# Attention's last product in plain fp32, with its transposed weights copied once

## The chip, the cores and the metric

The kernel runs on one core of a Trainium2 chip. A core has a matrix engine (TensorE, PE in the profile, its weight loads PEld), a vector engine (VectorE, DVE), an activation engine (ScalarE, ACT), a general engine (GpSimd, POOL) and an engine that issues most transfers (SyncE, SP). Each takes its instructions in the order in which the program wrote them, and waits on semaphores for the others. Matmul results land in PSUM, which VectorE and ScalarE read; the rest of the on-chip data is in SBUF. The metric is the time of one execution on the device, in microseconds (us), as the median of several runs.

## What is computed

A network of two layers on 1040 tokens (16 learned ones ahead of 1024 of the input) with 1024 features, all in fp32. Layer 0 mixes tokens by two parallel parts, a stick-breaking attention of 8 heads of 64 features and a state-space model (S5) with a gated unit behind it; layer 1 mixes by a gated delta rule; each layer ends in a wide MLP with squared ReLU. The change touches the attention alone:

```python
def block(args):
    qb, bi = args
    q_pos = bi * SB_BLOCK + jnp.arange(SB_BLOCK)
    valid = (key_pos[None, :] < q_pos[:, None]) & (key_pos[None, :] >= pad)
    z = jnp.einsum('bhqd,bhkd->bhqk', qb, kh) * scale
    log_keep = jnp.where(valid, jax.nn.log_sigmoid(-z), 0.0)
    log_surv = lax.cumsum(log_keep, axis=3, reverse=True) - log_keep
    w = jnp.exp(jnp.where(valid, jax.nn.log_sigmoid(z) + log_surv, -jnp.inf))
    return jnp.einsum('bhqk,bhkd->bhqd', w, vh)
```

The last line, weights times values, is what the change does in another way.

## The kernel before

**Number format.** Large products run in fp32r, a form of fp32 that TensorE multiplies at reduced precision. To keep fp32 accuracy each operand is split exactly into a part `hi`, rounded to fp32r, and a remainder `lo`, and three products hi x hi, hi x lo and lo x hi are summed in PSUM (`unit`, lines 174 to 176; the split itself is `split`, lines 222 to 230, a cast on ScalarE and a subtraction on VectorE or GpSimd). A few small products, those of S5 among them (lines 674, 715, 717), run in plain fp32 without a split.

**Order of the work.** `mixer0` (line 955) writes the program of layer 0. A main strand makes the S5 inputs, the values, the queries and keys, then calls `attention`, then the output product. Side strands (the four quarters of S5, `s5_quarter`, and the gated unit `glu` with the first half of the output product) are generators; `tick` writes a piece of them after each unit of the main strand, and some of them pause until a rough count of TensorE's time, `self.clock`, has gone on by so much. So each engine's order is fixed when the program is built, and S5 and the gated unit are interleaved with the attention.

**Attention.** Heads are taken in four pairs p (128 features, one tile), queries in four pairs pr of tiles of 128 (the 16 extra tokens go with the first pair). That makes 4 x 4 x 2 = 32 units (p, pr, head). For each unit `weights` (line 828) makes the scores with three products (lines 845 to 847) and a mask (849), takes two sigmoids of them on ScalarE (851, 852), runs a reversed running product along the keys on VectorE (853), and multiplies the two on VectorE or GpSimd (854). The weights are then [queries, keys]. Four units later (`AHEAD` = 4) `outputs` (line 866) takes them up:

- The keys go by blocks (the 16 extra tokens, then 128 each): 2 pr + 3 blocks for a unit, in groups of one and then two, pr + 2 groups, so 8 x (2 + 3 + 4 + 5) = 112 groups in all.
- `group` transposes the weights of its blocks on TensorE into a PSUM tile `tr` (line 881; there are three such tiles).
- ScalarE rounds the transposed weights to `th` (line 890), VectorE makes the remainder `tl` (line 891). Both are scratch tiles from a ring of ten.
- `products` multiplies them by the values. The values of a block lie as 64 columns of hi beside 64 of lo, so one product of the 128 columns with `th` gives hi x hi in 64 partitions and lo x hi in the other 64 (line 899), and a second one, of the 64 hi columns with `tl`, adds to the former (line 900). `later` holds a group's products back behind the transposes of the next three groups (`DEP` = 3).
- `store` copies one half of the result on ScalarE (line 913) and adds the other on VectorE (line 914).

`load_v` (line 811) fetches the values of a pair of heads into a raw buffer (`wraw`, two of them, which all weight loads share) and splits them, hi on ScalarE, lo on GpSimd. For the next pair it is called ahead of the last unit of the present one.

Of the kernel before, what the change touches and what calls it, by code (L numbers as in the profile page):

```python
# [44 lines left out]
def f(ap):  # L45
    return ap.bitcast(F32)


class Net:
# [6 lines left out]
    def step(self, strand):  # L56
        """emit the next piece of a strand; whether there was one that need not wait"""
        self.busy, was = True, self.busy
        going = False
        while strand:  # L60
            try:
                going = next(strand[0]) is not WAIT
                break
            except StopIteration:
                strand.pop(0)
        self.busy = was
        return going

    def tick(self, n=1):
        """emit n more pieces of the work that runs beside the present one, of its strands in turn"""  # L70
# [24 lines left out]
    def until(self, name, strand=None):  # L95
        """emit of a strand, or of all, up to what is named"""
        while name not in self.done:
            if strand is None or not self.step(strand):
                self.clock += 0.5
                self.tick()  # L100
# [12 lines left out]
    def pause(self, us):  # L113
        """wait while the tensor engine is given work for some time"""
# [35 lines left out]
    def weight(self, src, n=1024, spare=False, fast=False):  # L150
        """a weight tile as hi + lo; spare: in slots, beside the weights in use"""
# [15 lines left out]
    def unit(self, pt, kts, wap, rhs, o, n):  # L167
        """One output tile [128, n]: three passes of split products over kts."""
# [25 lines left out]
    def rowscale(self, cols, n, nsub, invd):  # L194
        """cols(j): [128, sub] summands whose sum over partitions is wanted per token; returns
        1/sqrt(sum * invd + eps) in a PSUM tile [128, nsub * sub], the same in every partition."""
# [10 lines left out]
    def spread(self, r, sub, nsub):  # L207
        """[sub, nsub] per-token values to rows that every partition holds."""
# [13 lines left out]
    def split(self, hi, lo, src, gain=None, lo_eng=None):  # L222
        """hi + lo = src (* gain per partition) exactly."""
# [8 lines left out]
    def norm_in(self, st, m, c, chunks, hsn, gcol):  # L232
        """Account one piece of the residual stream for the next product: its square sum, and the
        piece times the norm's gain as hi + lo."""
# [21 lines left out]
    def pieces(self, src, c, chunks, eng, mid=None):  # L256
        """a chunk of a [128, 8, tokens] stream, some feature tiles to a slot"""
# [11 lines left out]
    def first_norm(self):  # L269
        """the first norm, of all but the first chunk in pieces beside the first product"""  # L270
# [29 lines left out]
    def residual(self, acc, ssq, reuse, gpost, hs_old, gpre, chunks):  # L300
        """hs + rms(acc) * gain, and what the next norm or the output takes of it. Returns a hook for
        the last product before it, which goes by chunks of tokens: a chunk is taken up while the next
        one is made. reuse gives its place to the next state."""
# [65 lines left out]
    def mlp(self, layer, st, hs_d, chunks, gpre, ahead=None):  # L369
        """gpre: the next norm's gain column, or None at the end."""  # L370
# [79 lines left out]
    def s5_params(self):  # L450
# [24 lines left out]
        # powers 0..8 of exp(lambda dt), [128, 9, 16]  # L475
# [17 lines left out]
        # decay of a chunk and its rotation, as unit vectors 1, 2, 4 .. 128 chunks on  # L493
# [14 lines left out]
        # coef = (abar - 1) / lambda  # L508
# [15 lines left out]
        # bbar over b, -c_re and -c_im beside c  # L524
# [17 lines left out]
        # rotation tables over chunks, pairs 0..7 and 8..15  # L542
# [30 lines left out]
    def s5_mats(self, q):  # L573
        """Matrices of the groups 8 q .. 8 q + 7 for chunks of 8 tokens: inputs to state, inputs to
        outputs, and the state before the chunk to outputs."""
# [34 lines left out]
        # impulse response, then the Toeplitz matrices by reading it at shifted places  # L610
# [22 lines left out]
    def s5_ready(self, ud):  # L633
        """what the quarters need, back on chip, a quarter ahead"""
# [30 lines left out]
    def s5_quarter(self, q, ud):  # L665
# [21 lines left out]
        def rotate(dst, src, sign):  # L687
            """dst = src * exp(sign i phi)"""
# [59 lines left out]
    def glu(self):  # L748
        """gelu(y) * sigmoid(gelu(y) w + b), in place, with its square sum"""
# [34 lines left out]
    def normed(self, tiles, ssq, gcol, reuse=None):  # L784
        """rms norm over the features of 4 tiles, as hi + lo"""
# [11 lines left out]
    def attention(self, qd, kd, vd, vd0):  # L797
        """stick-breaking attention, by pairs of heads (a tile of features) and pairs of query tiles"""
# [12 lines left out]
        def load_v(p):  # L811
            cols = slice(128 * p, 128 * p + 128)
            raw = self.raw()
            nc.sync.dma_start(raw[:, :1024].rearrange("p (k d) -> p k d", k=8), vd[:, :, cols].rearrange("k p d -> p k d"))
            r0 = self.small([16, 128], "v0r", bufs=1)
            nc.sync.dma_start(r0, vd0[:, cols])
            # for a head and a block of keys, hi beside lo
            v0 = self.small([16, 2, 2, 64], "v0", F32R)
            self.split(v0[:, :, 0], v0[:, :, 1], r0.rearrange("p (h d) -> p h d", h=2), lo_eng=nc.gpsimd)
            V = []  # L820
            for h in range(2):
                t = self.slot("vv", F32R)
                t4 = t[:, :1024].rearrange("p (k s d) -> p k s d", k=8, s=2)
                self.split(t4[:, :, 0], t4[:, :, 1], raw[:, :1024].rearrange("p (k h d) -> p k h d", k=8, h=2)[:, :, h], lo_eng=nc.gpsimd)
                V.append([v0[:, h].rearrange("p s d -> p (s d)")] + [t[:, 128 * i:128 * i + 128] for i in range(8)])
            return V

        def weights(qk, h, i, kp=None, sg=None):
            """[q, keys] weights of q tile i"""
# [27 lines left out]
        pend = []  # L857
        self.ssq_sb = self.slot("ssqsb")

        def later(item, depth=DEP):  # L860
            """products wait for their operands behind the transposes of the next groups"""
# [4 lines left out]
        def outputs(p, pr, h, w, V, osb):  # L866
            # blocks of keys: (index, first q column, q columns)
# [4 lines left out]
            def group(gr):  # L872
# [16 lines left out]
                th, tl = self.tmp("wth", F32R), self.tmp("wtl", F32R)  # L889
                nc.scalar.copy(th[:kn, :off], pt[:kn, :off])  # L890
                v.tensor_sub(tl[:kn, :off], pt[:kn, :off], f(th[:kn, :off]))

                def products():
# [3 lines left out]
                    for kb, c0, cn, at in place:  # L897
                        a, o = V[h][kb], av[0][:, c0:c0 + cn]
                        nc.tensor.matmul(o, a, th[:kn, at:at + cn], start=first, stop=False, skip_group_check=True)
                        nc.tensor.matmul(o[:64], a[:, :64], tl[:kn, at:at + cn], start=False, stop=kb == 2 * pr + 2 or c0 == 256, skip_group_check=True)  # L900
# [8 lines left out]
            def store():  # L909
                t0 = TT[2 * pr + 1][0]  # L910
                hp = slice(64 * h, 64 * h + 64)
                for t, c0, cn in ((t0, 0, 256), (0, 256, 16))[:2 if pr == 0 else 1]:
                    nc.scalar.copy(osb[hp, t:t + cn], av[0][0:64, c0:c0 + cn])
                    v.tensor_add(osb[hp, t:t + cn], av[0][64:128, c0:c0 + cn], osb[hp, t:t + cn])
# [40 lines left out]
    def mixer0(self, st, rows):  # L955
# [3 lines left out]
        # s5 inputs  # L959
# [22 lines left out]
        # token-wise scales for the products that have tokens in the partitions  # L982
# [7 lines left out]
        # values, tokens in the partitions  # L990
# [55 lines left out]
    def out_block(self, acc, w, ks, rhs, first, chunks, W=()):  # L1046
        """products of some feature tiles with the mixer's last weights"""
# [20 lines left out]
    def out_last(self, acc, W, ks, rhs, chunks, gpost, hs_d, gpre, ahead):  # L1068
        """the last of them, and the residual stream after it"""
# [19 lines left out]
    def token_col(self, pt, cols):  # L1089
        """cols(i): summands [128, tokens of tile i]; their sums per token, in column i of pt"""  # L1090
# [3 lines left out]
    def gates(self, st, rc):  # L1094
        """decays and write strengths of all heads, tokens in the partitions: [128, 9, 8]"""
# [74 lines left out]
    def take(self, t):  # L1170
        """weights of one tile of the input projection; loads those of the next one ahead"""
# [6 lines left out]
    def conv_in(self, st, tiles, order, hook=None):  # L1178
        """inputs of the causal convolution, for some tiles of 128 features"""
# [819 lines left out]
```

## Time and profile before

| what | us |
|---|---|
| median of 3 runs | 3023.68 (3019.16 to 3024.05) |
| span of the profiled execution | 3011.3 |
| attention within it: first score product to last store | 290 to 653 |
| line 891, VectorE's remainder, busy in all | 61.9 |
| line 890, ScalarE's cast, busy in all | 53.2 |

The profile is of one execution. Its span runs from the first instruction to the last; the time of a run also holds what lies before and after, and the profile gives no other total for its execution. Busy times of an engine are sums over its instructions; those of TensorE are of overlapping matmuls with modelled ends, so a busy TensorE need not be one at its peak. The granted clock is the share of its full clock that TensorE was given.

### The profile page before, as it was taken

How to read it: one execution, taken by the hardware profiler on the slowest of the kernel's cores; microseconds unless marked ns; L12 is line 12 of the kernel's file. 1: busy time of each engine (PE TensorE's matmuls, PEld its weight loads, DVE VectorE, ACT ScalarE, POOL GpSimd, SP SyncE). 2: the span in 40 equal slices, each digit the busy share in tenths (PEclk: the TensorE clock that was granted, in tenths of full speed). 3: DMA queues.
4: the chain of work that ended last, by engine and by line, in shares of the span. 5: the costliest groups of instructions: out<-in, count | busy, mean ns of one | idle time of the engine just before them, and what ended most of it. 6: DMA issues, size and time to landing. Idle time of an engine off the chain costs nothing. (4 is left out here: it accounts for less than half of the span.)

```text
span 3011.3 us, 44561 instructions
## 1 busy us (share of the span) xinstructions
PE 2838.4 (94%) x17628; PEld 2685.8 (89%) x17628; DVE 1773.1 (59%) x3158; ACT 892.8 (30%) x1934; POOL 864.6 (29%) x628
## 2 busy tenths in 40 slices
PE   7899998999999999999896978999989999999998
PEld 7688667888999999999886978899988999999997
DVE  8633778667455555555646995545546455555555
ACT  4112566554311101111435423334434111111112
POOL 5551225225311221222522132211143222122123
PEclk9989567889999999999998999999999999999999
DMA  3435212134111111111426666453332111111113
GB/s 126 158 127 161 71 43 92 41 104 146 58 50 43 50 46 46 50 42 51 130 85 201 220 205 208 157 153 110 127 106 84 50 50 43 50 50 43 50 50 112
DMA packets 168289, 284.92 MB, mean 95 GB/s; under 512 B 40880, under 2 KB 108672, under 8 KB 168080
## 3 DMA queue, kind: packets, MB, share of 16 engines
q1 hardware_dynamic: 164192, 277.38, 28.8%
q10 hardware_dynamic: 3888, 4.69, 0.4%
q8 instruction: 139, 2.28, 0.3%
q14 instruction: 70, 0.57, 0.1%
HBM read 204.80 MB, written 77.21 MB: 94 GB/s over the span
## 5 line engine op out<-in xcount | busy, mean ns | idle before, releaser
L174 PE MATMUL mm<-ahi,whi 128*128 128x344 f32 (+2 forms) x2592 | 862.4, 333 | 33.5 <-DVE cx L1189 22.1
L164 POOL TENSOR_TENSOR wlo<-wraw,whi 128x1024 fp32r<-128x1024 f32 x181 | 439.5, 2430 | 1504.1 <-DVE whi L163 1138.1
L176 PE MATMUL mm<-ahi,wlo 128*128 128x344 f32 (+2 forms) x2592 | 844.9, 326 | 1.8 <-DVE wlo L164 1.8
L175 PE MATMUL mm<-hl,whi 128*128 128x344 f32 (+4 forms) x1920 | 619.1, 322 | 0.0
L174 PEld LDWEIGHTS mm<-ahi,whi 128*128 128x128 f32 x2592 | 497.2, 192 | 41.7 <-DVE cx L1189 23.3
L176 PEld LDWEIGHTS mm<-ahi,wlo 128*128 128x128 f32 x2592 | 497.0, 192 | 4.5 <-DVE wlo L164 2.9
L176 PE MATMUL mm<-hh,wlo 128*128 128x344 f32 (+4 forms) x1536 | 492.8, 321 | 2.9 <-POOL wlo L164 2.9
L408 DVE TENSOR_TENSOR acc<-mm,acc 128x344 f32<-128x344 f32 (+4 forms) x672 | 343.9, 515 | 253.4 <-PE mm L176 253.4
L174 PE MATMUL mm<-hh,whi 128*128 128x344 f32 (+4 forms) x1536 | 492.0, 320 | 0.1
L385 ACT ACTIVATE t<-t 128x344 f32<-128x344 f32 (+2 forms) x192 | 94.4, 492 | 1093.7 <-DVE t L384 1093.7
L175 PEld LDWEIGHTS mm<-hl,whi 128*128 128x128 f32 x1920 | 363.8, 189 | 1.3 <-issue 0.6
L175 PE MATMUL mm<-ml,whi 128*128 128x344 f32 (+2 forms) x1056 | 340.1, 322 | 0.7 <-DVE ml L227 0.7
L163 DVE CAST whi<-wraw 128x1024 fp32r<-128x1024 f32 x181 | 180.0, 997 | 196.7 <-PE mm L175 160.6
L176 PEld LDWEIGHTS mm<-hh,wlo 128*128 128x128 f32 x1536 | 289.2, 188 | 3.8 <-POOL wlo L164 3.5
L174 PEld LDWEIGHTS mm<-hh,whi 128*128 128x128 f32 x1536 | 289.5, 188 | 0.9 <-DVE acc L408 0.3
L227 DVE TENSOR_TENSOR hl<-t,hh 128x344 fp32r<-128x344 f32 (+2 forms) x192 | 162.2, 845 | 166.6 <-ACT hh L226 165.5
L175 PE MATMUL mm<-mh,whi 128*128 128x344 f32 (+2 forms) x768 | 246.8, 321 | 0.0
L175 PEld LDWEIGHTS mm<-ml,whi 128*128 128x128 f32 x1056 | 199.7, 189 | 1.1 <-DVE ml L227 1.0
L384 DVE SCALAR_TENSOR_TENSOR t<-mm,rb 128x344 f32<-128x344 f32 (+2 forms) x192 | 98.5, 513 | 121.0 <-PE mm L176 121.0
L175 PEld LDWEIGHTS mm<-mh,whi 128*128 128x128 f32 x768 | 144.6, 188 | 0.5 <-issue 0.2
L175 PE MATMUL mm<-hh,whi 128*128 128x344 f32 (+2 forms) x384 | 126.7, 330 | 0.0
L853 DVE TENSOR_TENSOR_SCAN keep<-keep,cst 128x400 f32<-128x400 f32 (+5 forms) x72 | 95.5, 1338 | 45.8 <-ACT keep L851 45.4
(425 smaller groups left out, 4530.0 us busy)
## 6 DMA issues: line engine op xcount, KB each, us to landing
wraw<-w SPq DMA_DIRECT2D x128, 512.0 KB, 3.5
wraw<-wino SPq DMA_DIRECT2D x32, 512.0 KB, 3.7
dm<-dmd SPq DMA_DIRECT2D x16, 520.0 KB, 4.8
hsd<-hs SPq DMA_DIRECT2D x48, 172.0 KB, 1.8
wraw<-wine SPq DMA_DIRECT2D x12, 512.0 KB, 3.7
wraw<-qkd SPq DMA_DIRECT2D x8, 520.0 KB, 3.6
acc<-acc SPq DMA_DIRECT2D x8, 520.0 KB, 4.6
dmd<-grow SPq DMA_DIRECT2D x8, 520.0 KB, 5.3
```

Source lines behind the costliest of these rows:

```text
L163: nc.vector.tensor_copy(hi[:, :n], raw[:, :n])
L164: (nc.vector if fast else nc.gpsimd).tensor_sub(lo[:, :n], raw[:, :n], f(hi[:, :n]))
L174: nc.tensor.matmul(pt, wh, h[:, o:o + n], start=i == 0, stop=False)
L175: nc.tensor.matmul(pt, wh, l[:, o:o + n], start=False, stop=False)
L176: nc.tensor.matmul(pt, wl, h[:, o:o + n], start=False, stop=i == len(kts) - 1)
L227: (lo_eng or nc.vector).tensor_sub(lo, src, f(hi))
L384: nc.vector.scalar_tensor_tensor(t1[:, :n], pt, 0.0, st["rb"][:, o:o + n], op0=ALU.max, op1=ALU.mult)
L385: nc.scalar.activation(t2[:, :n], t1[:, :n], AF.Square)
L408: nc.vector.tensor_add(acc[m][:, o:o + n], pt, acc[m][:, o:o + n])
L853: v.tensor_tensor_scan(kp[:n, 0:L][:, ::-1], kp[:n, 0:L][:, ::-1], self.one_row[:n, :L], 1.0, op0=ALU.mult, op1=ALU.mult)
```

## The change

The transposed weights are copied once, as plain fp32, to one scratch tile, on ScalarE for two groups of three and on VectorE for the third (`TURN` = 3). One plain fp32 product of a block's 64 value columns with them takes the place of the two split ones. The values are no longer split: they are fetched into one slot for both heads and used from there. The result stands in 64 partitions, so that one copy on VectorE stores it. Transposes, groups, `DEP`, the order in which pieces are written and `self.clock` are as before. The diff also takes out docstrings and comments.

```diff
@@ load_v
-            raw = self.raw()
-            nc.sync.dma_start(raw[:, :1024].rearrange("p (k d) -> p k d", k=8), vd[:, :, cols].rearrange("k p d -> p k d"))
-            r0 = self.small([16, 128], "v0r", bufs=1)
-            nc.sync.dma_start(r0, vd0[:, cols])
-            v0 = self.small([16, 2, 2, 64], "v0", F32R)
-            self.split(v0[:, :, 0], v0[:, :, 1], r0.rearrange("p (h d) -> p h d", h=2), lo_eng=nc.gpsimd)
+            t = self.slot("vv")
+            nc.sync.dma_start(t[:, :1024].rearrange("p (k d) -> p k d", k=8), vd[:, :, cols].rearrange("k p d -> p k d"))
+            v0 = self.small([16, 128], "v0")
+            nc.sync.dma_start(v0, vd0[:, cols])
             V = []
             for h in range(2):
-                t = self.slot("vv", F32R)
-                t4 = t[:, :1024].rearrange("p (k s d) -> p k s d", k=8, s=2)
-                self.split(t4[:, :, 0], t4[:, :, 1], raw[:, :1024].rearrange("p (k h d) -> p k h d", k=8, h=2)[:, :, h], lo_eng=nc.gpsimd)
-                V.append([v0[:, h].rearrange("p s d -> p (s d)")] + [t[:, 128 * i:128 * i + 128] for i in range(8)])
+                V.append([v0[:, 64 * h:64 * h + 64]] + [t[:, 128 * i + 64 * h:128 * i + 64 * h + 64] for i in range(8)])
             return V
...
@@ outputs, group
-                th, tl = self.tmp("wth", F32R), self.tmp("wtl", F32R)
-                nc.scalar.copy(th[:kn, :off], pt[:kn, :off])
-                v.tensor_sub(tl[:kn, :off], pt[:kn, :off], f(th[:kn, :off]))
+                wt = self.tmp("wt")
+                self.turn += 1
+                if self.turn % TURN:
+                    nc.scalar.copy(wt[:kn, :off], pt[:kn, :off])
+                else:
+                    v.tensor_copy(wt[:kn, :off], pt[:kn, :off])
...
@@ outputs, products
-                        a, o = V[h][kb], av[0][:, c0:c0 + cn]
-                        nc.tensor.matmul(o, a, th[:kn, at:at + cn], start=first, stop=False, skip_group_check=True)
-                        nc.tensor.matmul(o[:64], a[:, :64], tl[:kn, at:at + cn], start=False, stop=kb == 2 * pr + 2 or c0 == 256, skip_group_check=True)
+                        last = kb == 2 * pr + 2 or c0 == 256
+                        nc.tensor.matmul(av[0][:64, c0:c0 + cn], V[h][kb], wt[:kn, at:at + cn], start=first, stop=last, skip_group_check=True)
                         first = False
...
@@ outputs, store
-                    nc.scalar.copy(osb[hp, t:t + cn], av[0][0:64, c0:c0 + cn])
-                    v.tensor_add(osb[hp, t:t + cn], av[0][64:128, c0:c0 + cn], osb[hp, t:t + cn])
+                    v.tensor_copy(osb[hp, t:t + cn], av[0][0:64, c0:c0 + cn])
...
@@ parameters
+TURN = 3
```

More of the change, by code (lines that the diff above doesn't have):

```diff
@@ L857, in attention @@
         pend = []
+        self.turn = 0
         self.ssq_sb = self.slot("ssqsb")
```

## The prediction

> **What bounds the kernel now.** I began with the page: its head, the busy times, the slices.
>
> ```profile
> span 3011.3 us, 44561 instructions
> PE 2838.4 (94%) x17628; PEld 2685.8 (89%) x17628; DVE 1773.1 (59%) x3158; ACT 892.8 (30%) x1934; POOL 864.6 (29%) x628
> PE   7899998999999999999896978999989999999998
> DVE  8633778667455555555646995545546455555555
> PEclk9989567889999999999998999999999999999999
> ```
>
> TensorE (PE) is busy for 94% of the span. A slice is 75 us, so the fifth to ninth, about 300 to 675 us, are the attention, the only code that the change touches. They are the odd ones: PE is as full as elsewhere, but its granted clock is 0.5 to 0.8, and VectorE is busier than in most later slices. What the change is worth must be read there, not from the 94%.
>
> So next the busy times of the stretches of that stage. It runs from 290 us (first scores) to 653 us (last store). The columns are: length; PE, weight loads, VectorE, ScalarE, GpSimd, each with its instructions; granted clock; DMA share; GB/s.
>
> ```profile
> 290.00:370.00 80.00, 74.00 (x293) 53.36 (x292) 59.01 (x76) 48.39 (x124) 23.08 (x38) 0.58 0.30 83
> 370.00:450.00 80.00, 74.22 (x341) 55.32 (x339) 57.09 (x82) 45.29 (x112) 20.51 (x33) 0.67 0.17 54
> 450.00:530.00 80.00, 72.02 (x354) 57.57 (x353) 65.97 (x80) 49.25 (x112) 38.85 (x34) 0.74 0.28 87
> 530.00:610.00 80.00, 74.96 (x440) 63.88 (x440) 49.27 (x79) 47.08 (x107) 23.19 (x28) 0.91 0.13 45
> 610.00:653.00 43.00, 43.00 (x248) 33.78 (x246) 32.83 (x52) 26.00 (x62) 15.69 (x11) 0.80 0.20 62
> sum 363.00, PE 338.20 PEld 263.91 DVE 264.16 ACT 216.00 POOL 121.32; mean PE 67.64 PEld 52.78 DVE 52.83 ACT 43.20 POOL 24.26
> ```
>
> PE is busy for 338.2 of 363 us, VectorE for 264, ScalarE for 216. PE is idle for only 24.8 us. Weighted by length the clock is (80 x 0.58 + 80 x 0.67 + 80 x 0.74 + 80 x 0.91 + 43 x 0.80) / 363 = 0.734, so the stage holds 266 us of PE time at full clock. Who makes PE wait stands in the list of waits of this stretch:
>
> ```profile
> PE mm L845 <- ACT qkh L226: 5.7, 2, 4.6
> PE mm L174 <- ACT sig L852: 2.9, 1, 2.9
> PE ax L900 <- DVE wtl L891: 2.7, 2, 2.1
> PE ax L899 <- ACT wth L890: 1.6, 3, 1.2
> PE tr L881 <- DVE wtl L891: 1.3, 3, 0.5
> ```
>
> These are few and short: the two that concern VectorE's remainder and ScalarE's copy make 5.6 us. "Busy" flatters PE, though, since it includes the drain of each matmul. A score product that is followed by transposes shows it:
>
> ```profile
> 421.08 0.49 PE L847 MATMUL mm<-qkl,qkh 64*128 64x348 f32 x1
> 421.50 0.51 PEld L881 LDWEIGHTS tr<-cst,sig 128*128 128x128 f32 x3 [0.38 <-issue]
> ```
>
> The transposes' first weight load starts 0.42 us after the score product, while the products further down, of one form, follow each other in 0.12 us; it waits for no other engine. I read the stage as bound by PE's own stream, at a lowered clock, with 25 us of real waits in it.
>
> **The change, part by part: products.** The forms and the pace of the products, from the views of their tiles and from the timeline:
>
> ```profile
> L899 PE MATMUL ax<-wth,vv x160: 218/363/582, 318.6 to 651.0; 128*128 128x256 f32 x128, 128*128 128x128 f32 x32
> L899 PE MATMUL ax<-wth,v x40: 166/381/578, 311.2 to 648.2; 16*128 16x256 f32 x32, 16*128 16x16 f32 x8
> L900 PE MATMUL ax<-wtl,vv x160: 220/282/477, 319.0 to 651.1; 128*64 128x256 f32 x128, 128*64 128x128 f32 x32
> ...
> 641.91 0.28 PE L899 MATMUL ax<-wth,vv 128*128 128x256 f32 x1
> 642.03 0.28 PE L900 MATMUL ax<-wtl,vv 128*64 128x256 f32 x1
> 642.15 0.60 PE L881 MATMUL tr<-cst,sig 128*128 128x128 f32 x4
> ...
> 142.54 1.53 PE L674 MATMUL mm<-u,s5mt 128*128 128x130 f32 x12
> 143.83 0.48 PE L1002 MATMUL mm<-whi,ahi 128*128 128x512 f32 x1
> ```
>
> There are 160 + 40 = 200 blocks, each with one hi and one lo product. They stream 128 x 256 + 32 x 128 + 32 x 256 + 8 x 16 = 45184 columns, a mean of 226 per block. At full clock a 256-wide product takes 0.12 us from start to start (641.91, 642.03, 642.15), so a block costs 0.24 us. The new product is plain fp32, and its price shows in the state-space part, whose matmuls are plain fp32 already: the first six (the banks of three at line 674) appear as 12 records, two to a matmul, and take 143.83 - 142.54 = 1.29 us, 0.1075 us a record of 130 columns. For 256 columns that is 0.21 us a record, 0.42 us a block. The surcharge is 0.42 - 0.24 = 0.18 to 0.19 us for 256 columns, 0.168 us for the mean block, 200 x 0.168 = 33.6 us at full clock. The narrower weight (64 columns instead of 128 for the hi half) shortens only loads that run beside the matmuls; I cost it at nothing, and if loads showed, it would be a small gain.
>
> What it costs at the clock that is really granted follows from where the blocks lie:
>
> ```profile
> 290.00:370.00 80.00, 12.27 (x27) 7.85 (x27) 0.58 0.30 83
> 370.00:450.00 80.00, 18.84 (x49) 12.62 (x49) 0.67 0.17 54
> 450.00:530.00 80.00, 15.21 (x42) 9.98 (x42) 0.74 0.28 87
> 530.00:610.00 80.00, 11.86 (x35) 7.12 (x36) 0.91 0.13 45
> 610.00:653.00 43.00, 15.38 (x48) 9.81 (x47) 0.80 0.20 62
> ```
>
> This is line 899 alone (PE, weight loads). At the clocks of before, 0.168 x (27/0.58 + 49/0.67 + 42/0.74 + 35/0.91 + 48/0.80) = 46 us.
>
> **Copies and splits.** The groups of the same stretch, busy time and mean, then idle time before and its releaser:
>
> ```profile
> L891 DVE TENSOR_TENSOR wtl<-tr,wth 128x512 fp32r<-128x512 f32 (+3 forms) x112 | 61.9, 569 | 23.0 <-ACT wth L890 21.6
> L890 ACT CAST wth<-tr 128x512 fp32r<-128x512 f32 (+3 forms) x112 | 53.2, 490 | 39.6 <-PE tr L881 38.7 <-PE ax L900 0.2
> L914 DVE TENSOR_TENSOR osb<-ax,osb 64x256 f32<-64x256 f32 (+1 forms) x40 | 15.1, 377 | 5.7 <-ACT osb L913 4.6
> L913 ACT COPY osb<-ax 64x256 f32<-64x256 f32 (+1 forms) x40 | 12.9, 323 | 12.9 <-PE ax L900 8.1 <-DVE osb L914 4.3
> L227 POOL TENSOR_TENSOR vv<-wraw,vv 128x512 fp32r<-128x512 f32 x8 | 10.8, 1363 | 24.8 <-ACT vv L226 24.8
> L226 ACT CAST vv<-wraw 128x512 fp32r<-128x512 f32 x8 | 4.9, 638 | 0.0
> ```
>
> VectorE loses 112 remainders (61.9 us) and gains every third copy, 112 / 3 = 37. No such copy from PSUM is in the trace at this size; it lies between nothing and the remainder's 569 ns, which reads two operands, so 0 to 21 us, and I take 20. The store is one operation instead of two: at most its 15.1 us stay. Net on VectorE about -42 us. ScalarE loses 37 casts (18 us), the 40 store copies (12.9) and the value casts (4.9): -36 us. GpSimd loses 10.8 us, and the 24.8 us for which that work held up its queue and the gate multiplies of line 854 behind it. The values' DMA now goes into a slot rather than a raw buffer, so it waits on SP's queue for a free slot; the raw buffer comes free sooner for the weights' loads behind it. One scratch tile and one value slot fewer per use: no cost.
>
> None of these engines sets the stage's end while PE is 93% busy, so this relief is worth what PE waits for it: the 5.6 us of the rows above as the near end, most of the 24.8 us as the far end. I take 6: the largest waits are for the query and key splits, which stay. The new wait is that a third of the copies stands in VectorE's queue behind scans and state-space work, and products and the PSUM tile's reuse wait for it; but until now every group waited for ScalarE and then VectorE, so no group waits longer than it did.
>
> **The clock.** It is the part that I can't price from one row. Between the first two stretches the blocks rise from 27 to 49 and the clock from 0.58 to 0.67, 0.09 for 22 blocks. A plain fp32 block streams twice the passes, as though there were 27, 49, 42 and 35 more: by that slope +0.11, +0.20, +0.17 and +0.09 (it can't pass 1), 0.126 over the stage. But 450 to 530 us has fewer blocks than the stretch before it and a higher clock, so blocks explain only a part. The bounds are 0 and 0.126; I take a little over a third, 0.046, so 0.78.
>
> **The sum.** PE time at full clock 266 + 34 = 300 us; at 0.78 that is 385 us, +22; less 6 of waits, +16 us. The span would be 3027 us. The median of the runs, 3023.68 us, lies 12.4 us above the profiled span, which holds what is outside the first and last instruction; I add the 16 us to the median: 3040 us.
>
> **The rivals.** *The clock rises enough: faster.* Place: 290 to 530 us, where it is 0.58 to 0.74. Price: with 300 us of work, the stage takes 363 us at a clock of 0.826, or at 0.81 with the 6 us of waits gone; from there on the longer products pay for themselves. With the full 0.126, a clock of 0.86, the stage takes 349 us, -14, with the waits gone -20: 3004 us. For it: the slope above. Against it: the scores, with their drains, are unchanged and keep the clock low. The Trainium skill, "TensorE: Matmul & The Clock Gate", section "What's actually happening", says that the gate follows how busy PE has recently been, which speaks for this rival. The same page, Part 4, says that transposes do not count as busy in the same way, so that doubled products would weigh the more. Where transposes and products alternate with little else, the trace has a full clock:
>
> ```profile
> 640.00:645.00 5.00, 5.00 (x40) 4.15 (x39) 3.94 (x8) 3.43 (x9) 0.39 (x1) 1.00 0.61 196
> ```
>
> So such work can earn it; whether the mixed stretches cross the line no row says. Chance 0.17.
>
> *The clock stays: slower by all of it.* +46 less 6, 3064 us. For it: the first two stretches stay at 0.58 and 0.67 with a PE that is busy for 74 of 80 us, so being busy is not enough. Chance 0.15.
>
> *PE isn't the bound.* Drains hide waits, and the 42 us of VectorE count more than their 6; with all 24.8 us of idle time gone and the forecast's clock, 22 - 25 = -3, and at a clock of 0.80 12 - 25 = -13, 3011 us. Against it: the waits named for PE are few. Chance 0.10 for faster.
>
> *They cancel.* Any mix of clock and waits between these that leaves the time within 0.2%, 6 us: 3024 us. Chance 0.18.
>
> **How the numbers follow.** The forecast (6 to 35 us slower, 3040 us) has 0.40. Slower by over 0.2% is 0.40 + 0.15 = 0.55, within 0.2% (about what a measurement of this kernel can tell from no change) 0.18, faster 0.17 + 0.10 = 0.27. The range leaves out about a tenth on each side: 3004 us, the full clock gain, to 3070 us, somewhat above the case without any. The forecast's own range is 3030 to 3059 us.
>
> **What would show it.** In the changed trace: 400 records of the product with a start-to-start time near 0.21 us for 256 columns at full clock; 75 copies on ScalarE and 37 on VectorE; VectorE's busy time in the stage down by about 42 us; a stage of about 379 us at a clock near 0.78; and nothing new outside it. Between 635 and 650 us, where the clock is full already, the last four units of work (2 x 7 and 2 x 9 blocks) must lengthen by about 0.168 us a block, some 5 us; this part can't be given back by the clock. I am wrong if the stage's clock comes out above 0.81, or if PE's idle time in it falls by far more than 6 us.

## The result, and the profile after

| | median, us | runs |
|---|---|---|
| before | 3021.42 (3014.82 to 3024.05) | 4 |
| after | 3052.74 (3045.09 to 3057.49) | 4 |

The ratio is 1.0109, 95% interval 1.0087 to 1.0131: the changed kernel is some 31 us slower. The sign was forecast, about half of the size: +16 us had been predicted, 3040 us inside a range of 3004 to 3070.

The head of the page after, its busy times and the clock by slices:

```profile
span 3055.7 us, 44325 instructions
PE 2888.6 (95%) x17628; PEld 2677.4 (88%) x17628; DVE 1736.8 (57%) x3083; ACT 863.4 (28%) x1845; POOL 854.9 (28%) x616
PEclk9888687979999999999998989999999999999999
```

PE has as many records as before (two for a plain product, as for the two split ones), VectorE 75 instructions fewer. The clock's lowest slices still lie among the fifth to ninth (6, 8, 7, 9 and 7 tenths). The first score product now starts at 287 us and the last store ends at 682 us, 395 us for 363, so the stage holds +32 us, all of the difference of the medians. What lies outside it is 2648 us in the profiled run of before and 2661 us in that of after; in the eight experiments with plain products it lies between those two, so I read that difference as scatter from run to run (each of these figures is of one execution). The busy times of the stage by stretches (length; PE, weight loads, VectorE, ScalarE, GpSimd; granted clock; DMA share; GB/s):

```profile
288.00:368.00 80.00, 76.79 (x296) 46.17 (x296) 47.58 (x64) 41.63 (x103) 19.26 (x35) 0.66 0.30 82
368.00:448.00 80.00, 76.52 (x333) 47.20 (x333) 51.20 (x70) 40.40 (x95) 24.43 (x31) 0.77 0.16 49
448.00:528.00 80.00, 71.66 (x314) 46.14 (x315) 50.12 (x46) 37.17 (x77) 30.18 (x26) 0.81 0.22 72
528.00:608.00 80.00, 70.71 (x377) 54.22 (x377) 41.21 (x70) 36.83 (x83) 20.95 (x28) 0.91 0.15 47
608.00:682.00 74.00, 74.00 (x309) 44.94 (x308) 31.94 (x40) 29.28 (x67) 19.72 (x17) 0.77 0.15 48
sum 394.00, PE 369.68 PEld 238.67 DVE 222.04 ACT 185.31 POOL 114.54; mean PE 73.94 PEld 47.73 DVE 44.41 ACT 37.06 POOL 22.91
```

VectorE is down from 264 to 222 us, ScalarE from 216 to 185. Weighted by length the clock is 0.784 (0.734 before), so the stage holds 394 x 0.784 = 309 us at full clock, where it held 266. PE is idle for 394 - 369.7 = 24.3 us, as much as before. PE is longer at work, at a somewhat higher clock, and the relief of the other two engines has bought it no waiting time. The new groups on VectorE and ScalarE (busy, mean ns; idle before, and its releaser):

```profile
L887 ACT COPY wt<-tr 128x512 f32<-128x512 f32 (+3 forms) x75 | 35.6, 488 | 71.8 <-PE tr L876 71.6
L889 DVE COPY wt<-tr 128x512 f32<-128x512 f32 (+3 forms) x37 | 21.0, 566 | 40.5 <-PE tr L876 33.9 <-PE tr L880 6.0 <-DMA wraw<-w 0.6
```

What PE waits for in the stage (total, times, longest):

```profile
PE tr L876 <- DVE wt L889: 4.9, 1, 4.9
...
PE tr L876 <- ACT wt L887: 3.2, 1, 3.2
...
PE ax L897 <- ACT wt L887: 2.3, 2, 1.9
...
PE ax L897 <- DVE wt L889: 0.2, 1, 0.2
```

The waits for the copies make 4.9 + 3.2 + 2.3 + 0.2 = 10.6 us; the waits for the cast and the remainder made 5.6. The longest of all is new in its length: transposes (line 876) that wait for a PSUM tile which VectorE has yet to copy out (the longest wait of this kind took 0.5 us before). The timeline of VectorE shows why (start, duration):

```profile
450.78 2.48 DVE L848 TENSOR_TENSOR sig<-sig,keep 128x400 f32<-128x400 f32 x1
453.19 3.39 DVE L847 TENSOR_TENSOR_SCAN keep<-keep,cst 128x528 f32<-128x528 f32 x1
456.50 0.66 DVE L889 COPY wt<-tr 128x512 f32<-128x512 f32 x1
```

The copy of 0.66 us stands behind a multiply and a scan, 5.8 us of work in one queue. PE's transposes start at 457.21, after a stop of 4.95 us.

Last, PE's timeline near the end of the stage, at full clock, and behind it the row of before that follows four transposes at 642.15 us:

```profile
661.64 1.08 PE L897 MATMUL ax<-wt,vv 128*64 128x256 f32 x4
662.65 0.66 PE L876 MATMUL tr<-cst,sig 128*128 128x128 f32 x4
663.24 0.86 PE L897 MATMUL ax<-wt,vv 128*64 128x256 f32 x4
```

```profile
642.50 0.36 PE L899 MATMUL ax<-wth,vv 128*128 128x256 f32 x1
```

Four records of 256 columns take 662.65 - 661.64 = 1.01 us, against 4 x 0.21 = 0.85 expected, and four transposes are followed by a product after 0.59 us, where before it was 642.50 - 642.15 = 0.35. Both changes of form take longer than expected. What a whole turn of transposes and products loses is measured alone in m1, below.

### The profile page after: what moved, and what is told of

Same layout as the page of the kernel before. It is cut to its first block, busy times and chain, and to the rows that moved or that the text cites. A ratio compares the mean times of both kernels' runs of the same rounds, so it can differ in the third digit from the quotient of the medians.

```text
span 3055.7 us, 44325 instructions
## 1 busy us (share of the span) xinstructions
PE 2888.6 (95%) x17628; PEld 2677.4 (88%) x17628; DVE 1736.8 (57%) x3083; ACT 863.4 (28%) x1845; POOL 854.9 (28%) x616
```

## The experiments

Theory P, in the expectations, is the prediction's reading: the price of the longer products is what counts, the copies and VectorE's relief hardly matter. Its rivals look for the time in VectorE's load or in where the copies stand. Each time is a median, each ratio is to runs of the kernel before on the same chip.

**b1_products_only: the change without its copies.** All casts on ScalarE as before, and a subtraction on VectorE that nothing uses in the place of the remainder. The values and the store stay as changed.

```diff
-                if self.turn % TURN:
-                    nc.scalar.copy(wt[:kn, :off], pt[:kn, :off])
-                else:
-                    v.tensor_copy(wt[:kn, :off], pt[:kn, :off])
+                nc.scalar.copy(wt[:kn, :off], pt[:kn, :off])
+                tl = self.tmp("wtl")
+                v.tensor_sub(tl[:kn, :off], pt[:kn, :off], wt[:kn, :off])
```

> The changed kernel, but each group has its cast on ScalarE and a subtraction on VectorE as before the change (its result is not used), so that of the copies nothing is gained. Theory P (TensorE's stream is the bound: longer products and the drains around them): as slow as the changed kernel or slightly slower, 3050 to 3062 us. Rival R (the new waits for copies on VectorE are the cost): most of it goes back, 3020 to 3035 us. Rival V (VectorE's relief had hidden a larger cost of the products): 3065 to 3095 us.

**b2_copies_only: the change without its products.** Two split products, but one copy for a group, two on ScalarE and the third on VectorE.

```diff
@@ on the kernel before
+        self.turn = 0
...
-                th, tl = self.tmp("wth", F32R), self.tmp("wtl", F32R)
-                nc.scalar.copy(th[:kn, :off], pt[:kn, :off])
-                v.tensor_sub(tl[:kn, :off], pt[:kn, :off], f(th[:kn, :off]))
+                th = self.tmp("wth", F32R)
+                self.turn += 1
+                if self.turn % 3:
+                    nc.scalar.copy(th[:kn, :off], pt[:kn, :off])
+                else:
+                    v.tensor_copy(th[:kn, :off], pt[:kn, :off])
...
-                        nc.tensor.matmul(o[:64], a[:, :64], tl[:kn, at:at + cn], start=False, stop=kb == 2 * pr + 2 or c0 == 256, skip_group_check=True)
+                        nc.tensor.matmul(o[:64], a[:, :64], th[:kn, at:at + cn], start=False, stop=kb == 2 * pr + 2 or c0 == 256, skip_group_check=True)
...
-                    nc.scalar.copy(osb[hp, t:t + cn], av[0][0:64, c0:c0 + cn])
-                    v.tensor_add(osb[hp, t:t + cn], av[0][64:128, c0:c0 + cn], osb[hp, t:t + cn])
+                    v.tensor_copy(osb[hp, t:t + cn], av[0][0:64, c0:c0 + cn])
```

> The kernel before, with its two fp32r products, but with one copy per group on ScalarE and VectorE in turn, and one copy at the store; both products take the rounded weights, so the remainders of the weights and the lo part of the values are left out of the result. Theory P: TensorE has the same work, so within 6 us of before, 3009 to 3027 us, rather on the lower side. Rival V (VectorE's 42 us count): 2980 to 3003 us. Rival R: slower than before, 3027 to 3045 us.

b1 took 3053.5 us, ratio 1.0113 (1.0091 to 1.0135), and b2 3003.1 us, 0.9941 (0.9923 to 0.996). The whole stage of each as one stretch, b1 first:

```profile
284.00:680.00 396.00, 375.93 (x1638) 240.22 (x1637) 258.23 (x363) 200.81 (x462) 111.27 (x134) 0.78 0.20 61
```

```profile
289.00:630.00 341.00, 318.19 (x1642) 253.02 (x1642) 228.57 (x288) 187.76 (x434) 130.78 (x144) 0.76 0.23 71
```

PE's busy time times the granted clock, called PE's work below, hardly depends on waits: 375.9 x 0.78 = 293 us for b1, 242 for b2, 338.2 x 0.74 = 250 for before, 370.7 x 0.78 = 289 for after (from 287 us on). With the same copies plain products thus cost 293 - 250 = 43 us (b1 against before) or 289 - 242 = 47 us (after against b2) at full clock. The prediction had 34. The copies alone, on the split products, gain 18 us, three times what theory P allowed: a miss, at the edge of rival V's 2980 to 3003. And the two don't add: with plain products the same copies gain nothing (3053.5 to 3052.7).

The 18 us are not waiting time that PE got back. Its idle time is 22.8 us in b2 and was 24.8; the rest of the stage's 22 us lies in less work (242 us for 250) and a somewhat higher clock. PE's waits for the copies, b1 first:

```profile
PE tr L876 <- DVE wtl L888: 3.0, 4, 1.2
PE ax L896 <- ACT wt L886: 2.6, 2, 2.4
```

```profile
PE ax L903 <- ACT wth L893: 6.3, 2, 5.3
PE tr L882 <- DVE wth L895: 3.4, 1, 3.4
```

They make 5.6 us in b1, as much as in before, and 9.7 us in b2, which is 50 us faster than b1. So the sum of these waits doesn't tell a slow kernel from a fast one.

**a4_one_pass: one rounded product.** The changed kernel with weights and values cast to fp32r.

```diff
-                wt = self.tmp("wt")
+                wt = self.tmp("wt", F32R)
...
@@ load_v, in part
+            nc.scalar.copy(v0, r0)
+            nc.scalar.copy(t[:, :1024], raw[:, :1024])
```

> The changed kernel with weights and values rounded to fp32r, one single-pass product of 64 columns a block; both remainders are left out. Against before one pass of 45184 columns less, 19 to 23 us at full clock, and VectorE's relief. Theory P: 3021 - 23/0.75 = 2990 us, within 10. If TensorE is not the bound: 3010 to 3025 us.

It took 2985.7 us, ratio 0.989 (0.987 to 0.991), as theory P had it. Against the changed kernel half of the products' records and the plain format are gone: 67 us. Its stage:

```profile
289.00:616.00 327.00, 291.88 (x1444) 225.51 (x1443) 232.23 (x287) 185.31 (x429) 116.22 (x132) 0.74 0.23 72
```

PE's work is 291.9 x 0.74 = 216 us, 73 less than in the changed kernel, while PE is idle for longer, 35 us. The products are what PE's time in this stage hangs on.

**m1_forms: TensorE alone.** PE runs mixtures of the stage's matmuls from constant data, and no other engine takes part. `tr` is a transpose, `split` a block of two fp32r products (128 and 64 columns by 256), `plain` one of a plain fp32 product (64 columns by 256), `qk` three score products and the mask. For instance:

```python
for n in range(40):
    tr(4)
    split(2)
for n in range(30):
    tr(4)
    plain(2)
for n in range(30):
    tr(4)
    plain(4)
for n in range(30):
    qk(1)
```

> No network: TensorE alone runs, one after the other, stretches of the attention's instructions in fixed mixtures, with nothing to wait for (the two fp32r products of a block; the plain fp32 product; transposes; four transposes with two blocks of either kind; score triples with their mask; score triple, four transposes and two blocks of either kind). Passes theory: a plain fp32 block of 256 columns takes 0.42 us and a split block 0.24 us at full clock, and four transposes with two blocks take the sum of the parts. Drain theory: four transposes with two plain blocks take 0.3 to 0.5 us more than the sum (0.35 + 0.85 = 1.2 us), with two split blocks under 0.1 us more than theirs. Clock: if the granted clock follows how densely columns stream, score triples alone stand at 0.5 and products alone at 1.0; if transposes do not count, they alone stand at 0.5.

The timeline of PE, at a full clock: split blocks, transposes with split blocks, transposes with two and with four plain blocks, and scores, transposes and two blocks, split and then plain.

```profile
12.10 0.28 PE L1935 MATMUL P<-rnd 128*64 128x256 f32 x1
...
12.33 0.28 PE L1935 MATMUL P<-rnd 128*64 128x256 f32 x1
...
98.20 0.60 PE L1930 MATMUL T<-cst,raw 128*128 128x128 f32 x4
...
99.11 0.60 PE L1930 MATMUL T<-cst,raw 128*128 128x128 f32 x4
...
140.37 0.65 PE L1930 MATMUL T<-cst,raw 128*128 128x128 f32 x4
140.96 1.08 PE L1939 MATMUL P<-raw 128*64 128x256 f32 x4
141.96 0.66 PE L1930 MATMUL T<-cst,raw 128*128 128x128 f32 x4
...
201.73 0.66 PE L1930 MATMUL T<-cst,raw 128*128 128x128 f32 x4
...
204.19 0.66 PE L1930 MATMUL T<-cst,raw 128*128 128x128 f32 x4
...
308.43 0.74 PE L1944 MATMUL Q<-rnd 64*128 64x348 f32 x3
...
310.18 0.74 PE L1944 MATMUL Q<-rnd 64*128 64x348 f32 x3
...
349.91 0.74 PE L1944 MATMUL Q<-rnd 64*128 64x348 f32 x3
...
352.20 0.74 PE L1944 MATMUL Q<-rnd 64*128 64x348 f32 x3
```

A split block takes 0.23 us (12.10 to 12.33). Two more plain blocks lengthen the period from 141.96 - 140.37 = 1.59 to 204.19 - 201.73 = 2.46 us, 0.43 a block. So the surcharge, 0.43 - 0.23 = 0.20 us for 256 columns, is about what the prediction had (0.18 to 0.19). Transposes alone start every 0.107 us (149 in 16 us, the row from 64 to 80 us in the last section), so four take 0.43 us. Four transposes and two split blocks would then take 0.43 + 0.47 = 0.90 us, and they repeat every 0.91: nothing is lost. Four transposes and two plain blocks would take 0.43 + 0.86 = 1.29 us, and they repeat every 1.59: 0.30 us is lost at each pair of changes. (The expectations of m1 and a6 count four transposes as 0.35 us, the time from their start to that of the next product, and so come to 0.39.) With scores between, the period goes from 1.75 to 2.29 us, 0.54 for two blocks, 0.14 more than their surcharge. If each of the 112 groups met a pair of changes, that would be 16 us at the low end (0.14) and some 34 at the high one (0.30), beside the 34 for the products themselves. The stage's 43 to 47 us lie below that sum, 50 to 68, so not every group can meet this gap in full. In the order that PE ran, products and transposes stand side by side at some 156 places of the stage, not 224.

**a1_all_scalar: all 112 copies on ScalarE** (`TURN` = 1000 instead of 3).

> The changed kernel with all 112 copies on ScalarE. Theory P: no difference that can be measured to the changed kernel, 3047 to 3059 us. Rival R (copies behind scans on VectorE cost): 3030 to 3045 us. If ScalarE's 18 us more matter: 3060 to 3070 us.

**a3_pairs: products by two groups at a time.** They come a group later on average, and products and transposes take turns half as often as the kernel writes them. In the order that PE ran, products and transposes stand side by side at some 112 places of the stage instead of 156 (counted in the traces).

```diff
-            while len(pend) > depth:
-                pend.pop(0)()
+            if len(pend) > depth + 1:
+                pend.pop(0)()
+                pend.pop(0)()
```

> The changed kernel, with the held-back products taken two groups at a time, so that TensorE changes half as often between transposes and plain fp32 products. If the drains at these changes cost 9 to 15 us at full clock, half of it comes back, 6 to 10 us with the clock of the stage: 3041 to 3049 us. If the passes alone are the cost: 3053 us within 6. If products that come later hold things up: above 3059 us.

a1 took 3024.1 us, ratio 1.0005 (0.999 to 1.0021); a3 3016.0 us, 0.9988 (0.9975 to 1.0001). Each gives back nearly all that the change had cost, with the same plain products: theory P misses both. So do all other ranges, a1 by lying under rival R's, a3 under that of the drains. The stage of a1, then of a3:

```profile
286.00:655.00 369.00, 352.64 (x1628) 232.20 (x1628) 206.44 (x251) 199.79 (x462) 118.28 (x134) 0.82 0.22 65
```

```profile
287.00:647.00 360.00, 343.87 (x1636) 230.71 (x1635) 221.99 (x289) 184.23 (x426) 117.79 (x134) 0.85 0.22 67
```

PE's work is what it was (352.6 x 0.82 = 289, 343.9 x 0.85 = 292, after 289); a3, with fewer changes between products and transposes, has no less of it. PE's idle time is 16 us instead of 24, and the clock is 0.82 and 0.85 instead of 0.78. One place shows how the two can hang together. The stretches around the stop at 457 us, in the changed kernel and then in a1:

```profile
450.00:455.00 5.00, 2.27 (x14) 1.32 (x12) 4.90 (x3) 1.08 (x2) 5.00 (x4) 1.00 0.20 58
455.00:460.00 5.00, 2.79 (x8) 1.67 (x9) 3.13 (x4) 0.00 (x0) 1.58 (x2) 0.66 0.82 266
460.00:465.00 5.00, 5.00 (x17) 3.03 (x16) 1.06 (x2) 1.57 (x4) 0.00 (x0) 0.50 0.82 317
465.00:470.00 5.00, 5.00 (x18) 3.77 (x17) 1.76 (x2) 0.90 (x3) 1.23 (x4) 0.50 0.00 0
```

```profile
450.00:455.00 5.00, 5.00 (x30) 3.12 (x30) 0.42 (x1) 2.17 (x5) 0.97 (x4) 1.00 0.60 237
455.00:460.00 5.00, 5.00 (x27) 3.41 (x27) 0.00 (x0) 0.49 (x2) 0.00 (x0) 1.00 0.01 2
```

PE stops for 5 us, and then runs at half its clock for the next 10 and more: 17 and 18 matmuls in 5 us where a1 has 30 and 27. Here a wait is paid twice. But waits alone don't account for the clock: in the last of the changed kernel's stretches above, from 608 us on, PE is busy for all of the 74 us and has 0.77.

**b3_pairs: the same pairs in the kernel before.**

> The kernel before, with the held-back products taken two groups at a time. Control of a3: with fp32r products next to transposes there is little drain to save, so within 6 us of before, 3015 to 3027 us. If it gains as much as a3, the gain there is not one of plain fp32.

3012.5 us, ratio 0.9975 (0.9958 to 0.9992). That is some 8 us under before, and a little under the range expected. The pairs give 8 us to the split products and 37 to the plain ones, so most of what they take out came in with the change, in this arrangement of it.

**a6_later and a5_scalar_pairs: which of the two things that pairs do.** a6 holds each group's products, and the stores, back by one group more and doesn't pair them (`DEP` = 4, `DST` = 4 for 3 and 3); a5 has the pairs and all copies on ScalarE.

> The changed kernel with every product and store held back one group of transposes longer (four instead of three), popped one at a time, so that products and transposes alternate as often as in the changed kernel. It tells apart why popping the products in pairs gave back 37 us. Theory W (what costs is PE's wait for a copy that stands behind VectorE's scans; a later product has more time to get it): 3016 to 3030 us, a clock of 0.82 to 0.85 in the stage from 287 us on. Rival D (what counts is how often PE changes between plain fp32 products and transposes, 0.39 us a pair at full clock where it was measured alone; half the 112 changes are worth 22 us at full clock): no gain here, 3045 to 3057 us, a clock near 0.78.

> The changed kernel with all 112 copies on ScalarE and the products popped two at a time. Theory W: both edits take out the same waits, so together they give little more than one of them, 3010 to 3022 us. Rival D: the two edits take out different things (28 us of copies, 37 us of changes) and add up, 2985 to 3000 us.

a6: 3021.7 us, 0.9993 (0.9981 to 1.0005). a5: 3013.0 us, 0.9969 (0.9955 to 0.9983). Later products alone, with nearly as many changes of form as in the changed kernel (some 152 places), give back 31 of the 37 us, and the two edits together hardly more than one. Both times lie where theory W had them, and rival D fails in both. The stage of a6:

```profile
287.00:643.00 356.00, 337.28 (x1610) 222.34 (x1611) 223.39 (x281) 181.56 (x417) 121.29 (x134) 0.86 0.21 65
```

It does 337.3 x 0.86 = 290 us of work in 356 us, 7 us less than the stage of before needed for 250, and its idle time is 18.7 us, no smaller than a1's. What it has more of is clock. And here a stop is not paid twice in the way it was at 457 us. After a6's longest stop, 5.9 us until about 500 us, the full clock is back by 505 us:

```profile
505.00:510.00 5.00, 4.44 (x29) 3.73 (x29) 4.47 (x8) 2.74 (x10) 2.64 (x4) 1.00 0.48 138
```

**a2_all_vector: all copies on VectorE** (`TURN` = 1).

> The changed kernel with all 112 copies on VectorE instead of every third. Theory W: three times the copies behind scans, so at least the 29 us that every third one costs again and up to 60 us more, 3080 to 3115 us; VectorE's busy time in the stage near 265 us, a clock of 0.74 or less. Rival (the place of the copies doesn't matter, only VectorE's load does, and at 265 us of 395 it isn't full): 3048 to 3060 us.

3034.3 us, ratio 1.0037 (1.0022 to 1.0051): 18 us faster than the changed kernel, with three times as many copies on VectorE. Both expectations miss, and the simple form of theory W falls: it isn't the number of copies on VectorE that costs.

**a7_shifted and a8_half: chance or rule.** a7 starts the turn one group earlier (`self.turn = 1`), a8 gives VectorE every second copy (`TURN` = 2).

> The changed kernel with the turn started one group earlier: still 75 copies on ScalarE and 37 on VectorE, but it is now the 2nd, 5th, 8th ... copy that VectorE makes. It asks whether the copies shared between two queues cost what they do in general, or whether the 29 us come from a few chance meetings of a copy with a scan, such as the one at 457 us (4.95 us of waiting, 9 us behind the kernel with all copies on ScalarE by then). Theory G (shared in general, every group's chain runs through both queues): 3045 to 3057 us. Rival A (a few meetings, which another phase misses or finds elsewhere): 3015 to 3040 us, a clock of 0.80 or more in the stage.

> The changed kernel with every second copy on VectorE: 56 on each engine. Theory G: as slow as the changed kernel or somewhat slower, 3048 to 3065 us. Rival A: anywhere between 3015 and 3055 us, with no order by the number of copies on VectorE (0 gave 3024, 37 gave 3053, 112 gave 3034 us).

a7: 3034.4 us, 1.0042 (1.0028 to 1.0056). a8: 3036.4 us, 1.005 (1.0031 to 1.0069). The same 75 and 37 copies, one group apart, are 18 us faster, so theory G fails in both. The times lie in rival A's ranges, but that for a8, 3015 to 3055, was so wide that it says little. The phase of the turn counts; that it does so by meetings with scans is not shown. The stage of a7 does the same work (359.5 x 0.81 = 291 us) at a clock of 0.81 with 16.5 us of idle time:

```profile
287.00:663.00 376.00, 359.49 (x1628) 234.15 (x1628) 220.04 (x288) 185.60 (x425) 112.29 (x134) 0.81 0.21 64
```

All plain kernels together, in the order of the stage's clock. The time is the median; the other columns are of the one profiled execution, whose own time lay within 7 us of it.

| kernel | us | PE busy x clock, us | PE idle, us | clock |
|---|---|---|---|---|
| after; b1 | 3052.7; 3053.5 | 289; 293 | 24.3; 20.1 | 0.78 |
| all on VectorE; shifted; half | 3034.3; 3034.4; 3036.4 | 294; 291; 290 | 13.6; 16.5; 18.9 | 0.81 |
| all on ScalarE | 3024.1 | 289 | 16.4 | 0.82 |
| pairs; pairs and all on ScalarE | 3016.0; 3013.0 | 292; 293 | 16.1; 16.5 | 0.85 |
| one group later | 3021.7 | 290 | 18.7 | 0.86 |

The work varies by 5 us, the idle time by 11, the time by 40. Most of it is the clock that an arrangement happens to earn: from the changed kernel to a1 the stage shortens by 26 us, 18 in PE's busy time at the same work and 8 in its idle time. In the first six kernels of the table (all but the last two rows) PE's instructions are the same and written in the same order. Yet PE doesn't run them in the same order: building the program moves some of them, and it moves others when a copy changes its engine. Behind the mask of the same score (314.20 us in the changed kernel, 312.82 us in a7) PE goes on with a product in the changed kernel and with the next score in a7:

```profile
314.42 1.11 PE L897 MATMUL ax<-wt,v 16*64 16x256 f32 x2
```

```profile
313.04 0.66 PE L839 MATMUL mm<-qkh 64*128 64x348 f32 x1
```

So an arrangement is PE's own order as well as when each instruction can start, and these runs don't separate the two.

## Why the prediction was right or wrong

**The products' price: right in kind, too low.** The surcharge of a block is as worked out from the S5 rows (0.20 us measured alone, 0.18 to 0.19 predicted). The term of 33.6 us came out at 43 (b1 against before) and 47 (after against b2). A candidate for the missing 9 to 13 us is the gap where plain products and transposes change (0.14 to 0.30 us in m1), for which a row of S5 matmuls, all of one form, could not speak. That it makes up the difference is not shown: in a3 and a5, with some 112 and 110 places of change for 156, the gap would make 3 to 7 us less work of PE, but it is 292 and 293 us there and 289 in the changed kernel.

**The copies: this step failed.** "... until now every group waited for ScalarE and then VectorE, so no group waits longer than it did", and a relief worth 6 us. VectorE's busy time fell by 42 us as predicted, and the copy's price was right (21.0 us for 37, predicted 20). But waits for the copies rose from 5.6 to 10.6 us, and PE's idle time stayed (24.8 and 24.3): the 6 us did not come. The step counted the engines that a group waits for; at 457 us it was the place of a copy in VectorE's queue that cost PE 4.95 us. The measure itself, PE's waits, was wrong too. The copies alone gain 18 us (b2) with more waiting for them than before and 2.0 us less idle time, and b1, with as little waiting for its copies as before, is as slow as the changed kernel. Another phase of the turn is 18 us faster (a7), and 19 us faster than b1, which lacks most of the relief; but since arrangements differ by as much, no run separates what the relief is worth from what the phase does.

**The clock: right in size, by luck.** 0.78 was chosen between two bounds, and 0.784 came. But the same PE instructions earned 0.81 and 0.82 in other arrangements (a2, a7, a8, a1), so 0.78 doesn't follow from the denser products that the prediction argued from; it is what this phase of the turn gave. The bound of 0.126, a clock of 0.86, is where the changed kernel with later products ends (a6). For the rival "the clock rises enough" the break-even was put at 0.81 to 0.826 with 300 us of work; a1, with 0.82, stands at the time of before. Its price was too hopeful: at 0.85 and 0.86 one kernel with plain products is 9 us faster than before (a5), and two can't be told from it (a3, a6), not 20 us faster, for the products cost some 10 us more than it reckoned with.

**The sum.** Predicted: 300 / 0.78 = 385 us, less 6, a stage of 379. Measured: 309 / 0.784 = 394 us, and nothing to take off. The 15 us that the stage was missed by are 9 for the products and 6 for the relief that did not come. Both errors have the same sign, and the range was wide enough to hold them. How far the time moved is a matter of the phase: +31 us here, +13 with the same copies one group apart (a7). The check on the last units could not be made, since PE stood at half clock from 625 to 657 us, where it had been at full clock before.

**The step from span to median.** The prediction put the 12.4 us between the profiled span of before and the median down to what lies outside the first and last instruction. In the run after the span is 3055.7 us and that run's own time 3057.49: only 1.8 us lie outside. With as little outside, the profiled run of before took some 8 us less than the median one. Adding the difference to the median, not to the span, kept this from the forecast.

What stays open: what holds the clock at 0.5 where PE doesn't stop, and so why one arrangement earns 0.78 and another 0.86. Score products are a lead. In m1 they run at half clock when alone (last section), and in the changed kernel they fill 7.4 of the 40 us up to 624 us, at full clock, and 13.5 of the next 34 us, at half clock (the score products' time on PE, the clock, DMA):

```profile
584.00:624.00 40.00, 7.43 (x32) 1.00 0.14 49
624.00:658.00 34.00, 13.53 (x33) 0.50 0.05 16
```

No run moves the scores alone, so this is not shown. Even one program doesn't always earn the same: of a1's twelve runs the shortest took 3010.5 us with a clock of 0.961 over its whole span, the longest 3032.0 us with 0.951. Open too is why b2's PE work is 8 us below that of before with the same products.

## What to carry to other kernels

Price a change of format by the new form's rows, and then ask what follows it on the engine: a row of one form doesn't show the gaps at changes of form. Where a lowered clock bounds a stage, try two or three neutral placements of a changed piece (another phase, one group later) before judging it: here the same work took 3013 to 3053 us. Compare PE's order too, since a copy that goes to another engine can move matmuls. Of the kernels that compute everything, before with pairs (3012.5 us) and plain products with pairs and all copies on ScalarE (3013.0 us) are the fastest, both some 0.3% ahead of before.

## What the runs showed of the hardware that was not expected

The granted clock doesn't follow from PE being busy alone. In m1 the score products with the mask, 64 rows deep and back to back, ran alone at half clock, and transposes alone at full clock; PE is busy all the time in both (m1's stretches: length; PE, weight loads, VectorE, GpSimd; clock, DMA share, GB/s):

```profile
64.00:80.00 16.00, 16.00 (x149) 16.00 (x148) 0.00 (x0) 0.00 (x0) 1.00 0.00 1
250.00:280.00 30.00, 30.00 (x88) 19.48 (x88) 0.00 (x0) 0.00 (x0) 0.50 0.00 1
340.00:380.00 40.00, 40.00 (x210) 23.73 (x209) 0.00 (x0) 0.00 (x0) 1.00 0.00 1
```

The last row is scores with transposes and plain products between: full clock again, as with split products between (300 to 325 us, 1.00 too). The Trainium skill, "TensorE: Matmul & The Clock Gate", Part 4, says that transposes don't count as busy in the same way and that the full clock doesn't engage for them. The 16 us of transposes alone at 1.00, which PE entered at full clock, speak against it for fp32 transposes as this kernel makes them. Of the clock theories in m1's expectation the one by which transposes don't count thus fails.

A VectorE copy out of PSUM costs what a subtraction with a second operand does (566 and 569 ns for the mean group); ScalarE's copy takes 488 ns.
